# Own tiles for some early weights, own PSUM banks for the channel transform, and layer 1's first queries beside its latent keys

## Chip, core and metric

One core of one Trainium2 chip runs a forward pass of two layers in one launch. The metric is the device time of one execution in microseconds (us). Before the change the median of three runs is 1389.44 us (1386.45 to 1392.38).

## What is computed

Each of the two layers takes 256 latent tokens `x` and 256 context tokens `xc` of width 1024, in fp32:

```python
h = modulate(x, g_norm1, sh1, sc1)          # rms_norm * (1 + scale) + shift, from silu(c) @ w_mod
proj = h @ w_in                             # keys/values (288+ cols), queries, Fourier input, three gates
o_mla  = attention(q_mla, k_mla, v_mla)     # 8 heads, latent attention with a rotary key
o_gqa  = attention(q_gqa, k_gqa, v_gqa)     # 8 query heads on 2 key/value heads
o_four = real(fftn(f, axes=(tokens, channels of a group)))     # 4 groups of 128 channels
y = sig(g0)*(o_mla @ w_br_mla) + sig(g1)*(o_gqa @ w_br_gqa) + sig(g2)*(o_four @ w_four)
x = x + gt1 * (y @ w_o)
u = conv3(modulate(x, g_norm2, sh2, sc2) @ w_up)               # depthwise, width 3
x = x + gt2 * ((silu(a) * v) @ w_down)                         # a, v = halves of u
```

Context tokens go through the same weights with a constant conditioning vector; in layer 1 they only give keys and values. The output is `x` after layer 1.

## The kernel before

Activations lie feature-major, 128 features of all tokens to a tile. An fp32 product is three matmuls of rounded halves, hi·hi, hi·lo and lo·hi (`mm3`, L107 to L110), so each weight has to be split into a high and a low part before TensorE (PE) can use it. `wchunk` (L77 to L103) does that. The SP queue loads up to 512 KB into one of three `raw` buffers, ScalarE (ACT) casts the high part (L122), and VectorE (DVE) subtracts it from the weight to give the low part (L128). The results go into rings of three tiles, `whi` and `wlo`. Where a call names tiles of its own (`own`), they go there, and the ring is left free for others. SP issues in order, so a load waits for its `raw` buffer and everything behind it waits too.

The order of the instructions on each engine is set by a scheduler that simulates a timeline from the program and its priorities. Engines then run their lists strictly in order, PE's included. PSUM tiles come from five named groups: `mm`, `s` and `pt` with two banks each, `o` and `tk` with one each.

Names, in the order of a layer (the prefix `L0` or `L1` is the layer):

- `norm_mod` (L329): squares (`sq`, ACT), sums over features by PE (`ss`, L360), a reciprocal root on DVE in a dozen small steps, a diagonal `dg` (L369), its broadcast by PE (`rb`, L370), and then per feature tile `t` (DVE, L375), `h` high (ACT, L376) and `h` low (DVE L381, for every fourth tile ACT L378 and POOL L379). Stats and apply run for the latent half of the columns first, then for the context half.
- `kvg` (L527 on): keys and values of four token tiles, 288 columns each. Layer 1 does the two latent tiles first, then `q_chunk(0)` with its weights in tiles of their own, then the two context tiles, then `q_chunk(1)` (256 columns each, tiles `qg`). `fo`/`fp` is the projection for Fourier mixing.
- `Zc`, `Zs` (L633 to L650): the transform over channels, two products per group `b`, put together into `z` by DVE (L642, L643) and ACT (L639, L644). In layer 0 all `Zc` use `mm` and all `Zs` use `s`.
- `gk` and `KG` (L844 to L848): transposes of the GQA keys and their copies for attention.
- Gates `gp`, branch products `bp` with weights `b_w`; `gM`, `bM` are those of the MLA branch. `yh` is the split of the gated sum, `o` the output projection with weights `wo`.
- ConvFFN: `upp`, then `dp` with weights `dn`, in two groups of 12 and 10 hidden tiles in layer 0. Layer 1's modulation vectors are computed in the meantime: `sums` (L1016) runs steps of `mod_sums` (L283), each a load of 512 KB of `w_mod` (`mraw`, two buffers) and one DVE multiply-add (`mod_acc`, L298).
- `mod_burst` (L242): a quarter of one modulation block as products on PE (`mod_ps`, L259). Layer 1 runs two of them ahead of its first norm's context half, in the list `n1`, and two at its second norm, in `n2`.
- `next_norm` (L1180): layer 1's norm, begun inside layer 0's last down projection.

## Time and profile before

| | us |
|---|---|
| median of three runs | 1389.44 (1386.45 to 1392.38) |
| profiled execution, its own time | 1388.23 |
| its span, first to last instruction | 1386.4 |
| PE busy (share of the span) | 1339.8 (97%) |
| DVE, ACT, POOL busy | 949.8 (69%), 660.7 (48%), 334.4 (24%) |
| mean granted TensorE clock | 0.988 of full speed |

Times inside the program are us from the span's start. "Busy" is time with an instruction in flight; a wait is idle time of an engine, put down to what came last before it went on. PEclk is the granted TensorE clock as a share of 2.4 GHz, so 0.50 is the level of 1.2 GHz.

### The profile page before, as it was taken

The page shows a single profiled execution, that of the slowest core. Times are in us where ns is not written, and L with a number is a line of the kernel's source. Part 1 is how long each engine was busy: PE and PEld are TensorE (multiplying, and loading weights), DVE is VectorE, ACT ScalarE, POOL GpSimd, SP SyncE. Part 2 cuts the span into 40 slices and gives each one's busy share as a digit, 9 for nine tenths or more (in the row PEclk, how much of TensorE's full clock was granted, in tenths as well). Part 3 has the DMA queues.
Part 4 walks back from the last instruction along what each step waited for, and adds up shares of the span by engine and source line. Part 5 has one row for each costly group of instructions (what it writes and reads, how often), then busy time and mean ns, then how long its engine had stood idle before and what let it go on. Part 6 is the DMA issues. An engine that isn't in the chain of part 4 may idle for free.

```text
span 1386.4 us, 22211 instructions
## 1 busy us (share of the span) xinstructions
PE 1339.8 (97%) x8381; PEld 1171.6 (85%) x8381; DVE 949.8 (69%) x1686; ACT 660.7 (48%) x1166; POOL 334.4 (24%) x399
## 2 busy tenths in 40 slices
PE   6999999999999999999999999899998999899998
PEld 4887888877888789888788888888987998899998
DVE  4675755676654657777966667778788867788853
ACT  3534654435454335444214443355665664566642
POOL 2211232264322421111000102121244524012200
PEclk8999999999999999999999999999999999999999
DMA  9733343234311633434673346644425346456663
GB/s 320 252 92 107 110 152 105 64 108 114 102 62 47 241 114 103 137 94 149 197 258 119 110 129 201 197 127 121 138 66 152 92 121 204 132 177 184 185 193 119
DMA packets 160437, 197.40 MB, mean 142 GB/s; under 512 B 7080, under 2 KB 144858, under 8 KB 160330
## 3 DMA queue, kind: packets, MB, share of 16 engines
q1 hardware_dynamic: 159328, 195.32, 45.4%
q8 instruction: 66, 1.08, 0.3%
q0 software_dynamic: 864, 0.61, 0.3%
q14 instruction: 41, 0.34, 0.1%
q10 hardware_dynamic: 138, 0.04, 0.0%
HBM read 191.76 MB, written 3.15 MB: 141 GB/s over the span
## 4 chain that ended last, share of the span: by engine, by line
PE 86%; DVE 6%; issue 3%; DMA 2%; POOL 2%; ACT 1%; SPq 0%; DVEq 0%; ACTq 0%; POOLq 0%
PE L0upp L109 6%; PE L0upp L108 6%; PE L0upp L110 6%; PE L1upp L108 3%; PE L1upp L109 3%; PE L1upp L110 3%; PE L0gp L109 3%; PE L0gp L110 3%; PE L0gp L108 3%; PE L0dp L108 2%; PE L0dp L109 2%; PE L0dp L110 2%; PE L1gp L110 2%; PE L1dp L110 2%; PE L1dp L109 2%
## 5 line engine op out<-in xcount | busy, mean ns | idle before, releaser
L108 PE MATMUL L0upp<-L0n_h,L0up_h 128*128 128x512 f32 (+1 forms) x384 | 141.5, 372 | 1.1 <-ACT L0n_h L376 1.1
L109 PE MATMUL L0upp<-L0n_h,L0up_h 128*128 128x512 f32 (+1 forms) x384 | 142.5, 373 | 0.0
L110 PE MATMUL L0upp<-L0n_h,L0up_l 128*128 128x512 f32 (+1 forms) x384 | 139.1, 371 | 0.0
L108 PE MATMUL L1upp<-L1n_h,L1up_h 128*128 128x256 f32 x352 | 97.0, 287 | 1.1 <-ACT L1n_h L376 1.1
L110 PE MATMUL L1upp<-L1n_h,L1up_l 128*128 128x256 f32 x352 | 97.1, 285 | 0.0
L109 PE MATMUL L1upp<-L1n_h,L1up_h 128*128 128x256 f32 x352 | 96.5, 285 | 0.0
L1065 POOL TENSOR_TENSOR L0sg<-L0sg,L0u 128x512 f32<-128x512 f32 x22 | 29.6, 1343 | 273.9 <-DVE L0u L1042 273.9
L108 PEld LDWEIGHTS L0upp<-L0n_h,L0up_h 128*128 128x128 f32 x384 | 71.9, 188 | 14.4 <-ACT L0n_h L376 1.5
L109 PEld LDWEIGHTS L0upp<-L0n_h,L0up_h 128*128 128x128 f32 x384 | 72.2, 188 | 13.0 <-DVE L0n_t L375 0.4
L110 PEld LDWEIGHTS L0upp<-L0n_h,L0up_l 128*128 128x128 f32 x384 | 72.3, 188 | 12.5
L128 DVE TENSOR_TENSOR L0up_l<-L0up_w,L0up_h 128x1024 fp32r<-128x1024 f32 x44 | 59.2, 1347 | 34.2 <-ACT L0up_h L122 33.7
L122 ACT CAST L0up_h<-L0up_w 128x1024 fp32r<-128x1024 f32 x44 | 46.4, 1054 | 75.4 <-PE L0upp L109 52.1
L108 PE MATMUL L0gp<-L0n_h,L0g_h 128*128 128x512 f32 x192 | 76.4, 399 | 0.0
L109 PE MATMUL L0gp<-L0n_h,L0g_h 128*128 128x512 f32 x192 | 76.2, 397 | 0.0
L298 DVE SCALAR_TENSOR_TENSOR mod_acc<-mod_w,cpad,mod_acc 128x1024 f32<-128x1024 f32 x49 | 62.9, 1308 | 18.6 <-DMA mod_w<-in_w_mod_dram 18.4
L110 PE MATMUL L0gp<-L0n_h,L0g_l 128*128 128x512 f32 x192 | 75.2, 398 | 0.0
L110 PE MATMUL L0dp<-L0act,L0dn_l 128*128 128x512 f32 (+1 forms) x196 | 72.5, 370 | 0.8 <-DVE L0dn_l L128 0.8
L108 PE MATMUL L0dp<-L0act,L0dn_h 128*128 128x512 f32 (+1 forms) x196 | 72.6, 371 | 0.0
L109 PE MATMUL L0dp<-L0act,L0dn_h 128*128 128x512 f32 (+1 forms) x196 | 72.1, 368 | 0.0
L108 PEld LDWEIGHTS L1upp<-L1n_h,L1up_h 128*128 128x128 f32 x352 | 67.3, 196 | 1.8 <-ACT L1n_h L376 1.8
L128 DVE TENSOR_TENSOR L1up_l<-L1up_w,L1up_h 128x1024 fp32r<-128x1024 f32 x44 | 54.5, 1238 | 19.2 <-ACT L1up_h L122 17.8
L110 PEld LDWEIGHTS L1upp<-L1n_h,L1up_l 128*128 128x128 f32 x352 | 67.3, 194 | 0.0
(1564 smaller groups left out, 4278.9 us busy)
## 6 DMA issues: line engine op xcount, KB each, us to landing
mod_w<-in_w_mod_dram SPq DMA_DIRECT2D x96, 512.0 KB, 4.8
L0up_w<-in_w_up_dram SPq DMA_DIRECT2D x44, 512.0 KB, 3.6
L1up_w<-in_w_up_dram SPq DMA_DIRECT2D x44, 512.0 KB, 4.3
L0g_w<-in_w_in_dram SPq DMA_DIRECT2D x24, 512.0 KB, 3.7
L1g_w<-in_w_in_dram SPq DMA_DIRECT2D x24, 512.0 KB, 3.7
L0dn_w<-in_w_down_dram SPq DMA_DIRECT2D x20, 512.0 KB, 4.0
L1dn_w<-in_w_down_dram SPq DMA_DIRECT2D x16, 512.0 KB, 3.6
L0wo_w<-in_w_o_dram SPq DMA_DIRECT2D x8, 512.0 KB, 7.2
```

The lines of the kernel that those rows point to most:

```text
L108: nc.tensor.matmul(ps, lh, rh, start=start, stop=False)
L109: nc.tensor.matmul(ps, lh, rl, start=False, stop=False)
L110: last_mm[0] = nc.tensor.matmul(ps, ll, rh, start=False, stop=stop).ins
L122: nc.scalar.copy(hi, src)
L128: ins = nc.vector.tensor_sub(lo, src, f(hi))
L298: nc.vector.scalar_tensor_tensor(acc, raw, cv, acc, op0=ALU.mult, op1=ALU.add)
L1065: nc.gpsimd.tensor_mul(g[:, :TQ], g[:, :TQ], us[1][:, :TQ])
```

## The change

Five things are changed in the code.

1. Layer 0's channel transform takes `pt`, `o` and `tk` for groups 2 and 3, beside `mm` and `s`.
2. The last of the four `bM` weights, the first `wo` chunk and half of the second get tiles of their own, `H0` to `H7`, which hold layer 0's first normed activations until the last gate has read them.
3. Layer 1's first query weights are loaded in `next_norm`, into `Y0`, `Y1` and the two `mraw` buffers. The first queries of both latent tiles are computed feature tile by feature tile beside the latent keys, in the two `pt` banks. `dg` moves to another tag, and the list of the ConvFFN's slots changes to fit.
4. All four bursts of layer 1's block 5 run at its second norm, with eight tiles of their own; none is left at the first.
5. In the second up group of layer 0 two steps of the modulation sums run per pair of hidden tiles, where it was one.

```diff
@@ wchunk (own tiles; an own part may now be None, or in the mod weights' pool)
-            if own:
-                hi, lo = (S.tile([P, WMAX], F32R, tag=t, name=f"{name}_{x}{i}") for x, t in zip("hl", own[len(parts)]))
+            if own and own[len(parts)]:
+                hi, lo = (wpool.tile([P, WMAX], F32R, tag=t, name=f"{name}_{x}{i}", bufs=2) if t == "mraw" else
+                          S.tile([P, WMAX], F32R, tag=t, name=f"{name}_{x}{i}") for x, t in zip("hl", own[len(parts)]))
...
@@ norm_mod, stats
-            dg = S.tile([P, 256], F32, tag=f"E{s}", name=f"{nm}_dg")
+            dg = S.tile([P, 512], F32, tag="of", name=f"{nm}_dg", bufs=2)[:, :256]
...
@@ layer, first projections
-            hs, seq, _ = norm
+            (hs, seq, _), wq0 = norm
...
+        def q_part(w, k, tt, ps):
+            ts = slice(tt * P, (tt + 1) * P)
+            wh, wl = w(k, 0, 256)
+            mm3(ps[:, :256], hs[k][:, 0, ts], hs[k][:, 1, ts], wh, wl, k == 0, k == KD - 1)
...
         for tts in ((0, 1), (2, 3)) if l else (range(4),):
+            psq = [pm(f"{n_}qg{tt}0", "pt") for tt in range(2)] if l and tts[0] == 0 else []
             for k in range(KD):
+                for tt, ps in enumerate(psq):
+                    q_part(wq0, k, tt, ps)
                 wh, wl = w3(k, 0, 288)
...
-            if l and tts[0] == 0:
-                q_chunk(0, ("pt", "pt"), [("B0", "B1"), ("B2", "D0")])
+            for tt, ps in enumerate(psq):
+                marks["qg0"] = wq0.last
+                q_done(0, tt, ps)
...
@@ layer, Fourier mixing
-            zc = pm(f"{n_}Zc{b}", "mm" if not last else "pt")[:, :260].rearrange("p (s k) -> p s k", s=2)
-            zs = pm(f"{n_}Zs{b}", "s" if not last else ("o", "tk")[b])[:, :256].rearrange("p (s k) -> p s k", s=2)
+            zc = pm(f"{n_}Zc{b}", "mm" if not last and b < 2 else "pt")[:, :260].rearrange("p (s k) -> p s k", s=2)
+            zs = pm(f"{n_}Zs{b}", ("s", "s", "o", "tk")[b + 2 * last])[:, :256].rearrange("p (s k) -> p s k", s=2)
...
@@ layer, merge and output projection
-            bM(mc, ("s", "mm", "pt", "s")[mc] if not last else ("s", "mm")[mc % 2])
+            bM(mc, ("s", "mm", "pt", "s")[mc] if not last else ("s", "mm")[mc % 2],
+               [("H0", "H1")] if mc == 3 and not last else None)
...
-            wos.append(wchunk(a["w_o"][l], 0, KD, mc * 256, 256, f"{n_}wo{mc}"))
+            wos.append(wchunk(a["w_o"][l], 0, KD, mc * 256, 256, f"{n_}wo{mc}",
+                              None if last else ([("H2", "H3"), ("H4", "H5")], [("H6", "H7"), None])[mc]))
...
@@ layer, ConvFFN
-        slots = ["B0", "B1", "B2", "B3", "D0", "D1", "D2", "D3", "D4", "Y0", "Y1", "E0", "E1"]
+        slots = ["B0", "B1", "B2", "B3", "D0", "D1", "D2", "D3", "D4", "E0", "E1", "Y0"]
...
-                    sums(1)
+                    sums(2 if j0 else 1)
...
@@ next_norm and the second layer's call
-        return n1
+        return n1, wchunk(a["w_in"][1], 0, KD, 928, 256, "L1qg0", [("Y0", "Y1"), ("mraw", "mraw")])
...
-        "n1": bursts(1, 5, (0, 1), ["Y1", "Y2", "Y3", "E1"], "pt"), "g": [], "m": [],
-        "n2": bursts(1, 5, (2, 3), free[8:12], "pt"), "f": [], "v": []}, [], None, nxt[0])
+        "n1": [], "g": [], "m": [], "n2": bursts(1, 5, range(4), free[8:], "pt"), "f": [], "v": []}, [], None, nxt[0])
```

What the scheduler makes of it, at three places. Line numbers in the rows of the change are those of the changed file, 1 to 14 higher.

ACT's list in layer 0's channel transform, before. `z` is the transform's result (L644 reads `Zc`, the buffer number tells the group), `KG` the GQA keys.

```order
L122 CAST L0fo_1224<-L0z_1220 128x512
L847 CAST L0KG_1279<-L0gk 64x512
L848 CAST L0KG_1279<-L0gk 64x512
L847 CAST L0KG_1280<-L0gk 64x512
L848 CAST L0KG_1280<-L0gk 64x512
L644 COPY L0z_1237<-L0Zc_1227 128x4
L639 COPY L0zt_1269<-L0Zs_1262 128x256
L644 COPY L0z_1254<-L0Zc_1244 128x4
```

After:

```order
L123 CAST L0fo_1224<-L0z_1220 128x512
L656 COPY L0z_1237<-L0Zc_1227 128x4
L651 COPY L0zt_1269<-L0Zs_1262 128x256
L123 CAST L0fo_1241<-L0z_1237 128x512
L656 COPY L0z_1254<-L0Zc_1244 128x4
L123 CAST L0fo_1258<-L0z_1254 128x512
L656 COPY L0z_1271<-L0Zc_1261 128x4
L123 CAST L0fo_1275<-L0z_1271 128x512
L859 CAST L0KG_1279<-L0gk 64x512
```

The key copies stood between group 0's and group 1's `z`; now they stand behind all four groups.

DVE's list at the end of layer 0's merge, before. `b_l` is the low part of the last branch weight, `gt` the gated product, `wo_l` output weights, and `yh` the first operand of the output projection.

```order
L128 TENSOR_TENSOR L0b_l_4738<-L0b_w_4735,L0b_h_4737 128x1024
L592 SCALAR_TENSOR_TENSOR L0gt_4243<-L0gt_4243,L0bp_0_4705 128x512
L592 SCALAR_TENSOR_TENSOR L0gt_4243<-L0gt_4243,L0bp_1_4706 128x512
L172 COPY cw_4771<-cw_p 128x88
L128 TENSOR_TENSOR L0wo_l_4823<-L0wo_w_4820,L0wo_h_4822 128x1024
L128 TENSOR_TENSOR L0wo_l_4829<-L0wo_w_4826,L0wo_h_4828 128x1024
L130 SCALAR_TENSOR_TENSOR L0yh_4784<-L0y_523,L0yh_4784 128x512
```

After:

```order
L129 TENSOR_TENSOR L0wo_l_4843<-L0wo_w_4840,L0wo_h_4842 128x1024
L604 SCALAR_TENSOR_TENSOR L0gt_4243<-L0gt_4243,L0bp_0_4705 128x512
L604 SCALAR_TENSOR_TENSOR L0gt_4243<-L0gt_4243,L0bp_1_4706 128x512
L173 COPY cw_4771<-cw_p 128x88
L129 TENSOR_TENSOR L0wo_l_4955<-L0wo_w_4952,L0wo_h_4954 128x1024
L129 TENSOR_TENSOR L0wo_l_4961<-L0wo_w_4958,L0wo_h_4960 128x1024
L131 SCALAR_TENSOR_TENSOR L0yh_4784<-L0y_523,L0yh_4784 128x512
```

The last branch weight and the first three output weights have moved further up; three later output weights have come to stand ahead of the first `yh`.

ACT's list from the last steps of layer 0 to layer 1's first norm, before (`qg_h` query weights, `h` the normed activations):

```order
L122 CAST L1qg_h_8514<-L1qg_w_8512 128x1024
L263 COPY mod_row_8405<-mod_ps_8392 128x256
L348 ACTIVATE L1n_sq_8329<-L0x_4811 128x256
L348 ACTIVATE L1n_sq_8331<-L0x_4811 128x256
L376 ACTIVATE L1n_h_8104<-L1n_t_8165,modT_186 128x256
L376 ACTIVATE L1n_h_8105<-L1n_t_8169,modT_186 128x256
L376 ACTIVATE L1n_h_8106<-L1n_t_8173,modT_186 128x256
L122 CAST L1qg_h_8520<-L1qg_w_8518 128x1024
L376 ACTIVATE L1n_h_8107<-L1n_t_8177,modT_186 128x256
```

After, first at the end of the down projection, where the cast of the first query weights stands between two casts of down weights:

```order
L123 CAST L0dn_h_8015<-L0dn_w_8013 128x1024
L310 COPY mod_row_7942<-mod_ps_7937 128x256
L123 CAST L1qg_h_8201<-L1qg_w_8199 128x1024
L123 CAST L0dn_h_8021<-L0dn_w_8019 128x1024
L123 CAST L0dn_h_8027<-L0dn_w_8025 128x512
```

and then at the norm itself:

```order
L123 CAST L1kvg_h_8439<-L1kvg_w_8437 128x576
L349 ACTIVATE L1n_sq_8341<-L0x_4811 128x256
L349 ACTIVATE L1n_sq_8343<-L0x_4811 128x256
L377 ACTIVATE L1n_h_8104<-L1n_t_8165,modT_186 128x256
L377 ACTIVATE L1n_h_8105<-L1n_t_8169,modT_186 128x256
L377 ACTIVATE L1n_h_8106<-L1n_t_8173,modT_186 128x256
L377 ACTIVATE L1n_h_8107<-L1n_t_8177,modT_186 128x256
L377 ACTIVATE L1n_h_8108<-L1n_t_8182,modT_186 128x256
```

Query casts no longer stand between the steps of the norm. On PE the products of queries and keys now alternate there by feature tile.

## Rows read from the trace of the kernel before

**Rows 1.** The page: busy time by engine; the chain that ended last, by engine

```profile
PE 1339.8 (97%) x8381; PEld 1171.6 (85%) x8381; DVE 949.8 (69%) x1686; ACT 660.7 (48%) x1166; POOL 334.4 (24%) x399
...
PE 86%; DVE 6%; issue 3%; DMA 2%; POOL 2%; ACT 1%; SPq 0%; DVEq 0%; ACTq 0%; POOLq 0%
```

**Rows 2.** PE's waits, whole span (for what: us in total, times, longest us)

```profile
PE L1kvg L108 <- ACT L1n_h L376: 2.6, 2, 1.4
...
PE L0Zc L108 <- ACT L0z L644: 2.6, 1, 2.6
...
PE L1n_rb L370 <- DVE L1n_dg L369: 2.2, 1, 2.2
...
PE L0o L109 <- DVE L0yh L130: 2.0, 1, 2.0
...
PE L0bp L110 <- DVE L0b_l L128: 1.8, 2, 1.2
...
PE L1kvg L110 <- POOL L1n_h L379: 1.5, 1, 1.5
...
PE L0dp L110 <- DVE L0dn_l L128: 0.8, 1, 0.8
```

**Rows 3.** Windows at L0's channel transform (the first row names the columns)

```profile
core 0: us, PE busy (x) PEld busy (x) DVE busy (x) ACT busy (x) POOL busy (x), PEclk, DMA share, GB/s
...
104.60:107.20 2.60, 0.02 (x1) 0.00 (x0) 1.53 (x4) 2.54 (x7) 0.00 (x0) 1.00 0.00 0
107.20:110.60 3.40, 3.37 (x9) 2.82 (x10) 3.24 (x6) 1.86 (x6) 1.58 (x2) 0.50 0.00 0
```

**Rows 4.** ACT by line, 103.5 to 107.3 (xcount, busy us, mean ns, idle before)

```profile
L848 ACT CAST L0KG<-L0gk 64x512 fp32r<-64x512 f32 x2 | 1.2, 580 | 0.0
```

**Rows 5.** Windows at the start of L0's output projection

```profile
462.70:465.40 2.70, 0.69 (x4) 0.32 (x2) 2.70 (x3) 2.06 (x3) 2.10 (x1) 1.00 0.92 330
465.40:469.00 3.60, 3.60 (x9) 2.81 (x10) 3.60 (x7) 0.07 (x1) 1.17 (x1) 0.53 1.03 320
```

**Rows 6.** DVE by line, 453.5 to 466

```profile
L128 DVE TENSOR_TENSOR L0wo_l<-L0wo_w,L0wo_h 128x1024 fp32r<-128x1024 f32 x2 | 4.4, 2254 | 0.0
...
L128 DVE TENSOR_TENSOR L0b_l<-L0b_w,L0b_h 128x1024 fp32r<-128x1024 f32 x1 | 2.0, 2009 | 0.0
```

**Rows 7.** DVE by line, 872 to 882.1

```profile
L298 DVE SCALAR_TENSOR_TENSOR mod_acc<-mod_w,cpad,mod_acc 128x1024 f32<-128x1024 f32 x3 | 4.3, 1440 | 1.7 <-DMA mod_w<-in_w_mod_dram 1.7
```

**Rows 8.** Windows from L0's last down product to L1's Fourier projection

```profile
890.90:895.20 4.30, 3.13 (x32) 2.14 (x31) 4.30 (x9) 3.56 (x8) 0.00 (x0) 1.00 0.57 190
895.20:900.70 5.50, 4.15 (x20) 3.91 (x19) 3.00 (x11) 1.69 (x4) 0.00 (x0) 0.69 1.01 312
900.70:907.90 7.20, 5.63 (x31) 5.40 (x32) 5.72 (x17) 3.40 (x8) 1.77 (x2) 0.76 0.39 112
...
920.00:929.20 9.20, 9.20 (x76) 9.20 (x75) 5.45 (x19) 4.49 (x9) 3.43 (x8) 1.00 0.54 142
```

**Rows 9.** ACT's waits, 888 to 906

```profile
ACT L1qg_h L122 <- DMA L1qg_w<-in_w_in_dram: 4.6, 2, 3.8
```

**Rows 10.** PE by line, 890 to 930

```profile
L259 PE MATMUL mod_ps<-mod_w,cpad 128*32 128x256 f32 x32 | 2.1, 385 | 0.0
```

**Rows 11.** Windows at L1's second norm

```profile
1181.30:1185.70 4.40, 1.91 (x19) 1.66 (x15) 3.79 (x17) 0.25 (x1) 0.00 (x0) 1.00 0.75 237
1185.70:1192.60 6.90, 5.78 (x24) 5.07 (x25) 5.49 (x14) 3.63 (x8) 0.73 (x1) 0.51 0.01 3
```

**Rows 12.** DVE by line, 1182 to 1186

```profile
L266 DVE TENSOR_TENSOR mod_row<-mod_row,mod_ps 128x256 f32<-128x256 f32 x2 | 0.8, 417 | 0.1
```

**Rows 13.** DMA issues, 885 to 905 (xcount, KB each, median us to landing)

```profile
L1qg_w<-in_w_in_dram SPq DMA_DIRECT2D x4, 512.0 KB, 4.5
```

**Rows 14.** The page's costliest groups: two whole-chunk weight splits

```profile
L128 DVE TENSOR_TENSOR L0up_l<-L0up_w,L0up_h 128x1024 fp32r<-128x1024 f32 x44 | 59.2, 1347 | 34.2 <-ACT L0up_h L122 33.7
...
L122 ACT CAST L0up_h<-L0up_w 128x1024 fp32r<-128x1024 f32 x44 | 46.4, 1054 | 75.4 <-PE L0upp L109 52.1
```

More of the change, by code (lines that the diff above doesn't have):

```diff
@@ L583, in gate, with branch @@
                          whole=lambda ps: nc.scalar.activation(packed[mc], ps, AF.Tanh, scale=0.5))
-            def branch(mc, bank=bank):
-                w = wchunk(a[wname][l], 0, 4, mc * 256, 256, f"{n_}b{b}{mc}")
+            def branch(mc, bank=bank, own=None):
+                w = wchunk(a[wname][l], 0, 4, mc * 256, 256, f"{n_}b{b}{mc}", own)
                 def gated(g, y, ps):
```

26 lines of the change are left out of this document (13 added, 13 removed).

## The prediction

> **What bounds the kernel now.** I read the page first. PE is busy for 97% of the span, and 86% of the chain that ended last is PE's [rows 1]. So a gain can come from three things only: products taken away, time in which PE stands idle, and time in which it runs at 1.2 GHz instead of 2.4. The change takes no products away, it only moves some. PE's waits come next. No single one is long. The places that the change touches show 2.6 us at layer 0's channel transform, 1.2 (the longer of two) and 2.0 at layer 0's merge and output projection, 0.8 in the last down projection, 2.6 and 1.5 at layer 1's keys, and 2.2 at layer 1's second norm [rows 2]. The windows then show what follows such a wait. After the 2.6 us at the transform, PE is busy for 3.37 of 3.40 us at a granted clock of 0.50 [rows 3]. Such a stretch delivers half its products, so it costs 1.7 us on top of the wait. The same shows after the wait at the output projection (0.53, [rows 5]), in two stretches at layer 1's keys (0.69 and 0.76, [rows 8]) and after its second norm (0.51, [rows 11]). So each wait is priced twice, as idle time and as clock.
>
> The profiled execution took 1388.23 us, of which 1386.4 are the span. The median of the runs is 1389.44, 1.2 above it. The sum is made on the trace and then taken off the median.
>
> **Part by part.**
>
> *Channel transform.* PE waits for L644, an ACT copy of four columns, and PE's own list is not at fault. Ahead of that copy on ACT stand the four key copies: the two of L848 take 0.58 each, those of L847 as much, together 2.3 us [rows 4]. The product that waits needs the bank which that copy frees. With banks of its own no group waits for another group's copy, and the key copies come behind all four `z`. The gain is at most 2.6 of wait and 1.7 of clock, 4.3. It is nothing at all if the first gate, which takes the next bank, waits instead. I take −3.5. PE gets 24 products and a gate without a stop, but the gate's first bank is still freed by ACT, which now has 2.3 us of key copies right behind, and I keep 0.8 for that.
>
> The Trainium skill speaks against it. In "TensorE: Matmul & The Clock Gate", in the section on how the clock oscillation bites in real kernels, a kernel whose products were already put in one run gained nothing further from PSUM double-buffering. By that page this part is 0 and the time 1381.6. The trace differs in one point, that the wait here ends with the copy that frees a bank [rows 2].
>
> *Merge and output projection of layer 0.* The last branch weight is split earlier, so the 1.2 us wait for `b_l` goes. But PE then only reaches the output projection sooner, and that waits for the first `yh`, which stands on DVE behind big splits. Before these were one `b_l` of 2.01 and two `wo_l` of 2.25 [rows 6]. Now they are three later `wo_l`. So the first `yh` is ready when it was, and the 2.0 us wait becomes 3.2. I take 0. The ends are −1.2 (`yh` comes earlier by that much) and +1.7 (the longer wait lengthens the stretch at half clock by one more). On SP seven `wo` loads now go ahead of the reloads of `x`. Those are first needed when a whole output group is done, and both kinds of load wait for tiles that come free earlier, so I cost that at nothing.
>
> *Last down projection.* Two steps of the modulation sums per pair of tiles bring the sums to an end earlier. DVE's `mod_acc` steps of 1.44 us [rows 7] then no longer stand ahead of the last down weights, and 0.8 of wait goes. A new wait comes: on ACT the copy of a modulation row, which needs a product at the end of the third quarter, now stands ahead of the cast of the first query weights, and that ahead of the fourth quarter's second down weights. Two casts of 1.05, and the split of 1.35 on DVE behind them [rows 14], with the copy (some 0.4, an estimate from the 256-column step of [rows 12]) make 3.9 us. The products in front that hide them are 24 of 256 columns, at 9.20/76 = 0.121 us each [rows 8] 2.9. So 1.0 shows. The term is +0.2, between −0.8 and +2.0 (both casts and the split bare).
>
> *Start of layer 1.* From 890.9 to 929.2 it takes 38.3 us [rows 8]. There PE has 96 query products of 256 columns, 0.121 each, 11.6 us, and 96 key products of 288 columns, by columns 0.136 (an estimate), 13.1. Two bursts of 2.1 us together [rows 10] leave. What the wait rows show is that ACT, in the middle of the norm, holds the cast of the second query weights and waits 3.8 us for their load [rows 9]. The activations behind it, and so PE, wait with it. In the new list that cast stands before the norm, its load goes ahead of most others, and each feature tile has 12 products (1.5 us) in place of 6. A DVE step on 256 columns takes 0.42 [rows 12] and a tile needs two, 0.84, so PE should set the pace once it has begun. Up to the first product there were 4.3 us, now 3.2 without the burst. The sum is 11.6 + 13.1 + 3.2, with one stretch at half clock (1.7, there were two) and the second half's broadcast (0.3), 29.9. So −8.4. The ends are −10.1 (no such stretch) and −2.1 (only the bursts leave, the norm sets the pace as before). The key weights are now loaded behind the queries, two of the context copies and the transform tables. They still have the down projection's fourth quarter to arrive, 120 products of 0.121, some 14 us, so I cost that at nothing. Without that cover a load costs up to 4.5 [rows 13].
>
> *Second norm of layer 1.* The two bursts come back here, 2.1 us. They stand behind the sums of squares and ahead of the broadcast, where PE is idle for 2.2 [rows 2] and is busy for 1.91 of 4.40 [rows 11]. They fill it. But DVE has two of the row additions inside its chain of small steps where both of the two stood ahead of it, each 0.42 [rows 12]. I take +0.4. The ends are −1.7 (PE no longer falls idle and half of the stretch at 0.51 goes) and +2.1 (nothing is hidden). Their loads, eight in place of four, go between the last branch weights on SP. Two tiles come free with each of the last two heads' scores, so SP is not held up long.
>
> *ConvFFN slots and the diagonal's tag* change no instruction's cost: 0.
>
> **Sum:** −3.5 + 0 + 0.2 − 8.4 + 0.4 = −11.3, 1376.9 for the profiled execution, 1378.1 for the median. All best ends together give −18.1, so 1371.
>
> **Rivals.**
>
> *The banks give nothing.* The wait moves to the first gate's bank: then −7.8, 1381.6. For it speaks that ACT is as busy there as it was (2.54 of 2.60 [rows 3]). Against it, the gate needs the bank only after all 24 products. By the skill's page above it would be so.
>
> *Query weights hold up the down projection.* The first of their two loads may start only when DVE has split the fourth quarter's first down weights, and if the sums' steps still stand there, it lands after that quarter has begun. Then ACT waits with the down weights behind it. A whole load of 4.5 [rows 13] and a stretch at half clock of 1.7 make +6.2, 1384. For it: the cast stands between two down casts. Against it: the sums are meant to end earlier.
>
> *Slower: attention of layer 0 runs out of cover.* The key copies go behind the transform, so the eight GQA heads start later, between gates and branch products as before, and yet have to be done by the same place. Where a head's softmax finds too few products beside it, PE waits. The nearest row is the wait in this same stretch, 2.6 and 1.7 of clock, 4.3 a head [rows 2, 3]. With three heads the gain is eaten (12.9 against 11.3), with four it is 1395. For it: every step of attention stands behind the moved copies. Against it: PE's table has no wait for layer 0's GQA heads among its larger ones, so there is cover to lose.
>
> **How the numbers follow.** A measurement of this kernel can tell about 0.5%, 6.9 us, from no change, so faster is below 1382.5. The forecast gets 0.62, the banks 0.12 (split about evenly by that line), the held-up down projection 0.14 (same), attention 0.05 (slower). Of the 0.07 left, in which the start of layer 1 gains little, nearly all is no change. That is 0.69 faster, 0.25 same, 0.06 slower. The range goes from 1371 to 1386, which takes in the second rival with the upper end of the merge's term.
>
> **What would show it.** The transform's wait on L644 is gone and the clock stays at 1.00 from 100 to 112. PE's wait for the first `yh` is over 3 us. The way from the last down product to the first Fourier product is near 30 us with at most one stretch at half clock, and ACT shows no wait for query weights within it. The second norm's wait is under 1 us. The forecast is wrong if the last down projection shows a wait of several us for down weights, if layer 1's keys and queries still wait for `h` at each tile, or if GQA heads of layer 0 appear in PE's waits.

## The result and the profile after

The changed kernel takes 1373.59 us (median of four runs, 1373.26 to 1375.59), beside 1389.09 for the kernel before in the same comparison (1386.45 to 1392.38). The ratio is 0.9894, with a 95% interval of 0.9877 to 0.9911. The time fell by 15.5 us where 11.3 were forecast, and lies in the range given, 1371 to 1386. The profiled execution has a span of 1371.5 us, 14.9 below that of before.

The page of the changed kernel, busy time by engine and the chain that ended last, by engine (as [rows 1]):

```profile
PE 1334.1 (97%) x8381; PEld 1168.4 (85%) x8381; DVE 949.2 (69%) x1686; ACT 660.1 (48%) x1166; POOL 335.0 (24%) x399
...
PE 89%; DVE 6%; DMA 2%; POOL 1%; issue 1%; ACT 1%; SPq 0%; ACTq 0%; DVEq 0%; POOLq 0%
```

PE has the same 8381 products, and its busy time fell by 5.7 us (1339.8 to 1334.1). A PE that does the same work in less busy time ran less of it at half clock. The rest of the gain is waiting that went.

PE's waits in the changed kernel, whole span (for what: us in total, times, longest us), as [rows 2]:

```profile
PE L0o L110 <- DVE L0yh L131: 3.5, 1, 3.5
...
PE L1n_ss L361 <- ACT L1n_sq L349: 1.1, 2, 0.7
...
PE L0gp L109 <- ACT L0gt L594: 1.1, 1, 1.1
...
PE mod_ps L275 <- DVE mod_row L267: 0.5, 1, 0.5
...
PE L1n_rb L371 <- DVE L1n_dg L370: 0.4, 1, 0.4
```

Gone are the 2.6 for `L0z`, the 1.2 for `b_l`, the 0.8 for `dn_l`, and all waits for `L1n_h` at layer 1's keys. The wait for `L1n_rb` fell from 2.2 to 0.4. That for the first `yh` rose from 2.0 to 3.5, and one is new, 1.1 for a gate's `gt`.

Windows of the changed kernel (the first row names the columns): the transform, as [rows 3]; the new wait of 1.1; the output projection, as [rows 5]; the start of layer 1, as [rows 8]; its second norm, as [rows 11]:

```profile
core 0: us, PE busy (x) PEld busy (x) DVE busy (x) ACT busy (x) POOL busy (x), PEclk, DMA share, GB/s
101.10:103.70 2.60, 2.60 (x23) 2.55 (x22) 2.52 (x5) 2.17 (x6) 0.00 (x0) 1.00 0.17 59
103.70:107.10 3.40, 3.38 (x19) 2.76 (x18) 3.38 (x9) 2.52 (x8) 0.00 (x0) 1.00 0.00 0
250.50:252.80 2.30, 1.27 (x11) 1.09 (x9) 1.11 (x9) 1.08 (x2) 0.36 (x1) 1.00 0.00 0
...
459.40:463.00 3.60, 0.20 (x2) 0.00 (x0) 3.60 (x3) 1.14 (x2) 3.05 (x2) 1.00 0.97 329
463.00:466.90 3.90, 3.84 (x10) 3.05 (x11) 3.90 (x6) 0.75 (x2) 1.66 (x1) 0.57 1.01 330
886.97:891.30 4.33, 3.20 (x21) 2.72 (x20) 4.33 (x10) 3.02 (x8) 0.00 (x0) 0.87 0.55 151
891.30:896.80 5.50, 5.50 (x37) 5.50 (x37) 5.40 (x23) 3.19 (x7) 0.74 (x1) 0.79 0.36 101
896.80:904.00 7.20, 7.20 (x58) 7.15 (x57) 3.84 (x11) 2.81 (x8) 1.02 (x2) 1.00 0.00 0
904.00:916.50 12.50, 12.50 (x101) 12.50 (x100) 9.84 (x29) 8.49 (x20) 6.47 (x11) 1.00 0.39 112
1168.50:1173.00 4.50, 3.56 (x46) 2.37 (x45) 3.83 (x18) 0.34 (x2) 0.00 (x0) 1.00 0.72 230
1173.00:1180.00 7.00, 5.88 (x44) 5.38 (x45) 5.96 (x16) 4.05 (x9) 0.74 (x1) 1.00 0.01 2
```

At the transform the 3.4 us that held 9 products at 0.50 now hold 19 at 1.00, with no idle time ahead. After the second norm 7.0 us hold 44 products at 1.00, where 6.9 held 24 at 0.51. The start of layer 1 keeps one dip, 0.87 and 0.79 in a row, and PE is never idle from 891.3 on. Of these places only the output projection still shows the old picture, a wait and then 10 products in 3.9 us at 0.57.

**Where the 15 us went.** PE works through its list in order, so the start of the same product in two traces tells how far one is ahead. The table gives, for every kernel of this study, how much longer (+) or shorter (−) a stretch between two such products is than in the changed kernel. The stretches are: up to the last key product of layer 0 (*start-up*); from there to the first gate product (*transform*); to the last `ukv` product (*latent*); to the last product of the output projection (*merge*); to layer 0's last `dp` (*down*); to the first `L1fp` (*L1 start*); to the first `L1upp` (*L1 rest*); to the last `L1upp` (*norm 2*). So *L1 rest* takes in the second norm itself, and *norm 2* is the up projection right behind it. What comes after it is equal in all of them to 0.05.

| kernel | start-up | transform | latent | merge | down | L1 start | L1 rest | norm 2 | sum |
|---|---|---|---|---|---|---|---|---|---|
| before | −0.6 | +4.1 | −0.9 | −0.1 | +1.3 | +9.0 | +0.3 | +1.9 | +15.0 |
| z_alone | −1.3 | 0 | 0 | −0.2 | +1.6 | +9.6 | +0.1 | +2.2 | +12.1 |
| bursts_alone | −0.6 | +4.0 | −0.8 | −0.1 | +1.1 | +3.7 | +1.3 | 0 | +8.4 |
| two_edits | −0.3 | 0 | 0 | −0.1 | +2.3 | +3.6 | +1.5 | 0 | +7.0 |
| z_undone | −0.3 | +3.9 | −0.8 | −0.1 | +1.6 | +0.2 | +1.5 | 0 | +6.0 |
| own_undone | −2.5 | 0 | 0 | −0.1 | +0.5 | +1.5 | +1.4 | 0 | +0.9 |
| sums_undone | −1.8 | 0 | 0 | −0.1 | +6.2 | +0.2 | +0.4 | +1.1 | +6.0 |
| bursts_back | +0.2 | 0 | 0 | −1.9 | −0.1 | +3.2 | +2.7 | +2.4 | +6.4 |
| q_behind | −2.5 | 0 | 0 | 0 | −0.1 | 0 | 0 | 0 | −2.6 |
| q_forced | −1.4 | 0 | +0.1 | −0.2 | +0.1 | +0.5 | +0.3 | 0 | −0.6 |
| q_late | −2.9 | 0 | +0.6 | −0.2 | 0 | +1.0 | +1.6 | 0 | +0.1 |
| yh_first | +0.4 | 0 | +1.6 | −4.9 | +0.1 | 0 | +0.3 | 0 | −2.6 |
| best | +0.2 | 0 | −1.1 | −4.1 | +0.1 | +2.4 | +0.3 | 0 | −2.2 |

The start-up differs by up to 3.3 us from trace to trace, and no edit touches it. So a total of one execution is worth little here, and the stretches are what the experiments are read by. They have a limit too: behind the same waits PE's clock is not the same in every execution, which by itself moves a stretch by up to some 2 us (the last section).

### The profile page after: what moved, and what is told of

Read it like the earlier page. It is cut to its first block, busy times and chain, and to the rows that moved or that the text cites. A ratio compares the mean times of both kernels' runs of the same rounds, so it can differ in the third digit from the quotient of the medians.

```text
span 1371.5 us, 22227 instructions
## 1 busy us (share of the span) xinstructions
PE 1334.1 (97%) x8381; PEld 1168.4 (85%) x8381; DVE 949.2 (69%) x1686; ACT 660.1 (48%) x1166; POOL 335.0 (24%) x399
## 4 chain that ended last, share of the span: by engine, by line
PE 89%; DVE 6%; DMA 2%; POOL 1%; issue 1%; ACT 1%; SPq 0%; ACTq 0%; DVEq 0%; POOLq 0%
PE L0upp L109 6%; PE L0upp L110 6%; PE L0upp L111 6%; PE L1upp L109 3%; PE L1upp L110 3%; PE L1upp L111 3%; PE L0dp L109 3%; PE L0dp L111 3%; PE L0dp L110 3%; PE L0gp L109 3%; PE L0gp L111 3%; PE L0gp L110 3%; PE L1dp L111 2%; PE L1dp L110 2%; PE L1dp L109 2%; PE L0bp L111 1%
## 5 line engine op out<-in xcount | busy, mean ns | idle before, releaser
L1079 POOL TENSOR_TENSOR L0sg<-L0sg,L0u 128x512 f32<-128x512 f32 x22 | 29.6, 1345 | 274.1 <-DVE L0u L1056 274.1
L109 PEld LDWEIGHTS L0upp<-L0n_h,L0up_h 128*128 128x128 f32 x384 | 71.9, 188 | 14.3 <-ACT L0n_h L377 1.5
L110 PEld LDWEIGHTS L0upp<-L0n_h,L0up_h 128*128 128x128 f32 x384 | 72.2, 188 | 13.0 <-DVE L0n_t L376 0.4
L129 DVE TENSOR_TENSOR L0up_l<-L0up_w,L0up_h 128x1024 fp32r<-128x1024 f32 x44 | 59.2, 1348 | 32.1 <-ACT L0up_h L123 31.6
L109 PEld LDWEIGHTS L1upp<-L1n_h,L1up_h 128*128 128x128 f32 x352 | 65.9, 192 | 1.5 <-ACT L1n_h L377 1.5
L110 PEld LDWEIGHTS L1upp<-L1n_h,L1up_h 128*128 128x128 f32 x352 | 66.2, 192 | 0.1
```

The lines of the kernel that those rows point to most:

```text
L109: nc.tensor.matmul(ps, lh, rh, start=start, stop=False)
L110: nc.tensor.matmul(ps, lh, rl, start=False, stop=False)
L129: ins = nc.vector.tensor_sub(lo, src, f(hi))
L1079: nc.gpsimd.tensor_mul(g[:, :TQ], g[:, :TQ], us[1][:, :TQ])
```

## Experiments

### The channel transform's banks

**z_alone**, on the kernel before:

```diff
-            zc = pm(f"{n_}Zc{b}", "mm" if not last else "pt")[:, :260]...
-            zs = pm(f"{n_}Zs{b}", "s" if not last else ("o", "tk")[b])[:, :256]...
+            zc = pm(f"{n_}Zc{b}", "mm" if not last and b < 2 else "pt")[:, :260]...
+            zs = pm(f"{n_}Zs{b}", ("s", "s", "o", "tk")[b + 2 * last])[:, :256]...
```

> The kernel before with the banks of the channel transform alone (groups 2 and 3 in `pt`, `o` and `tk`). Theory (the banks take the 2.6 us wait and the stretch at half clock behind it): PE shows no wait for `L0z`, the clock stays at 1.00 from 100 to 112, the first gate product starts at 104.6 where it was 108.0, and the execution takes about 1385.2, 3.1 less than 1388.2. Rival (the wait moves to the first gate's bank, or double-buffering gives nothing): the first gate product starts at 107 to 108 and the time is within 1 us of 1388. A second question: in the changed kernel a wait of 1.1 for the gate's `gt` stands at 251.8. If the banks alone bring it (the key copies behind the transform shift the later order), it shows here too and the gain at the first latent query product is 2.5; if another part of the change brings it, it is absent and the gain there is 3.5.

It took 1385.35 us, with a span of 1383.5. Its window at the transform, where the wait and the half clock were:

```profile
102.40:105.80 3.40, 3.37 (x19) 2.75 (x18) 3.37 (x9) 2.52 (x8) 0.00 (x0) 1.00 0.00 0
```

Among PE's waits, whole span:

```profile
PE L0gp L108 <- ACT L0gt L582: 1.1, 1, 1.1
```

And ACT's longest wait from 240 to 256:

```profile
ACT L0cqsq L723 <- PE L0ckss L735: 3.8, 1, 3.8
```

The first gate product comes 51.1 us after the last key product, as in the changed kernel, and 55.2 in the kernel before. So the banks take 4.1 from this stretch, nearly all of the 4.3 that the wait and the stretch at half clock cost. They bring the wait of 1.1 too. ACT's row tells how. It stands for 3.8 us before a square of the latent queries (`cqsq`) whose buffer PE has not yet read out (it is one of three that the key squares have before it, and `ckss` are the sums of these), and the gate's `gt`, for which PE waits, is behind that square on ACT. PE stops for a bank that ACT is to free, with ACT waiting for PE. The net gain at the last `ukv` is 3.1.

**z_undone**, the same two lines put back in the changed kernel:

> The changed kernel with the channel transform in `mm` and `s` alone, as before. Theory (the term is its own, independent of the others): the wait of 2.6 for `L0z` is back, with a stretch at about 0.5 of the clock, the first gate product starts at 108.0, the 1.1 at 251.8 is gone, and the execution takes 2.5 to 3.5 more than the changed kernel's 1373.6, about 1376.7. Rival (what is lost here is made up later, because the attention of layer 0 has slack that ends at the same place): the way up to the last GQA head is later by 3 but the output projection of layer 0 starts within 1 us of 458.9.

It took 1379.26 us. Its windows at the transform:

```profile
104.80:107.40 2.60, 0.13 (x2) 0.00 (x0) 1.42 (x4) 2.54 (x7) 0.00 (x0) 1.00 0.00 0
107.40:110.80 3.40, 3.26 (x10) 2.68 (x11) 3.32 (x6) 1.86 (x7) 1.58 (x2) 0.55 0.00 0
```

PE's waits, at the transform and in the last down projection:

```profile
PE L0Zc L109 <- ACT L0z L656: 2.6, 1, 2.6
...
PE mod_ps L307 <- DVE mod_acc L299: 1.0, 1, 1.0
```

The wait of 2.6 and the stretch at half clock (0.55) are back. The term is its own: +3.9 and −0.8, 3.1 net, and nothing of it is made up before the output projection. The total is 5.7 over the changed kernel's, where 3.5 at most was expected. The difference lies far from the edit: 1.6 in the down projection, where PE waits 1.0 for the modulation sums (the second row) after DVE has waited 2.6 for one of their loads (0.3 in the changed kernel), and 1.5 in the rest of layer 1, of which the last section tells.

### The tiles of their own in layer 0's merge

**own_undone**, on the changed kernel:

```diff
-               [("H0", "H1")] if mc == 3 and not last else None)
+               None)
...
-                              None if last else ([("H2", "H3"), ("H4", "H5")], [("H6", "H7"), None])[mc]))
+                              None))
```

> The changed kernel without tiles of their own for the last branch weight of layer 0 and the first output weights. Theory (the two waits trade places): the wait of 1.2 for `b_l` is back, the wait for the first `yh` falls from 3.5 to about 2.0, and the last output product comes within 0.5 us of where it was: 1373.6, give or take 0.7. Rival (the own tiles cost what the longer `yh` wait shows): 1.5 faster, 1372.1. Second rival (they are worth the `b_l` wait): 1.2 to 2.9 slower, up to 1376.5.

It took 1374.12 us. PE's waits from 440 to 520:

```profile
PE L0o L110 <- DVE L0yh L131: 2.0, 1, 2.0
PE L0bp L111 <- DVE L0b_l L129: 1.2, 1, 1.2
```

The two waits trade places to a tenth: the first output product comes 1.3 later against the stretch's start, the last one 0.1 earlier. By themselves these own tiles gain nothing here. They move a wait from the branch weight to `yh`. The 1.5 and 1.4 more at the start and in the rest of layer 1 come mostly from the clock, behind waits of the same length in all (the last section).

### Two steps of the sums per pair of tiles

**sums_undone**, on the changed kernel:

```diff
-                    sums(2 if j0 else 1)
+                    sums(1)
```

> The changed kernel with one step of the modulation sums per pair of hidden tiles in both up groups, as before. Theory (ending the sums earlier is what took the two waits of 0.8 and 0.3 out of the last down projection): those waits come back, the way from the first to the last down product is longer by about 1.3, and the time is 1374.9. Rival (the cast of the first query weights now waits for the `mraw` buffers that the sums still hold, with down weights behind it): 4 to 6 more, 1378 to 1380, with a wait for `dn` of several us. Second rival (the waits went because layer 1's query weights took `Y0`, `Y1` and with them the ConvFFN's slots changed): no difference, 1373.6 within 0.5.

It took 1379.31 us. PE's waits from 870 to 892:

```profile
PE L1n_ss L361 <- POOL L1n_sa L354: 1.9, 1, 1.9
PE L0dp L109 <- DVE L0x L982: 1.1, 1, 1.1
PE L0dp L111 <- DVE L0dn_l L129: 0.3, 1, 0.3
```

The windows around them:

```profile
875.00:878.50 3.50, 1.94 (x13) 1.43 (x11) 3.41 (x6) 1.61 (x3) 1.67 (x3) 1.00 0.95 306
878.50:880.30 1.80, 0.04 (x1) 0.04 (x1) 1.80 (x3) 0.25 (x2) 1.80 (x2) 0.59 0.76 236
880.30:884.00 3.70, 3.70 (x19) 2.66 (x20) 0.11 (x1) 1.00 (x3) 0.59 (x1) 0.50 0.51 151
```

The down projection is 6.2 longer. That is 3.3 of waits and the rest mostly clock, with only 19 products in 3.7 us at 0.50. The price is that of the prediction's rival in which query weights hold up the down projection (+6.2), but ACT's waits for them say little: 4.3 before the first cast here, 4.2 in the changed kernel. The form is another, too: the down weights cost 0.3, and most comes from DVE, where two steps of the sums (1.3 each, at 874.0 and 877.0) stand among the residual's additions, for which PE and the norm's squares wait. So with the early query weights the sums must end earlier. Part of the 6.2 is there without those weights as well: the kernel before, with late weights and one step per pair, is 1.3 longer in this stretch, while `q_late` below, with late weights and two steps, is as short as the changed kernel. That comparison has the other edits in it, the ConvFFN's slots above all, and the steps were not tried alone on the kernel before.

### The start of layer 1

Four parts changed here: where the bursts stand, when the query weights come, in which order the queries are written, and how early their two `pt` banks are taken.

**bursts_back**, on the changed kernel:

```diff
-        "n1": [], "g": [], "m": [], "n2": bursts(1, 5, range(4), free[8:], "pt"), ...
+        "n1": bursts(1, 5, (0, 1), ["B0", "B1", "B2", "D0"], "pt"), "g": [], "m": [],
+        "n2": bursts(1, 5, (2, 3), free[8:12], "pt"), ...
```

> The changed kernel with two of block 5's four bursts again ahead of the context half of layer 1's first norm, and two at its second norm. Theory (at the first norm PE has too little time free for them, at the second they stand in its idle time): the way from the last down product to the first Fourier product goes from 29.6 to 31.7 (the 2.1 us of the two bursts in full), the wait for `L1n_rb` goes from 0.4 to about 2.2, with one stretch at half clock more, and the time is 1373.6 + 2.1 + 2.0 = 1377.7. Rival (at the first norm they now hide behind the feature tiles, and the second norm's gain has another cause): both places within 0.7 of the changed kernel, 1374.

It took 1379.67 us. PE's waits at the second norm, and, second row, at the start of layer 1:

```profile
PE L1n_rb L371 <- DVE L1n_dg L370: 2.2, 1, 2.2
...
PE mod_ps L260 <- DMA mod_w<-in_w_mod_dram: 1.4, 2, 0.7
```

The window behind the first:

```profile
1177.00:1184.00 7.00, 5.88 (x26) 5.48 (x27) 5.86 (x14) 4.02 (x9) 0.73 (x1) 0.56 0.01 3
```

Both places move the way the theory had it: the wait of 2.2 and the half clock (0.56) are back at the second norm, whose up products take 2.4 longer, and the start of layer 1 is 3.2 longer. That is the bursts' 2.1 and 1.1 more. PE waits 1.4 for their weights there and 0.4 for `L1n_h`, but no longer the 1.1 for the squares, which is 0.7 of it. The total is about 2 above the theory's: 1.1 and 0.4 at these two places, 2.7 more in the rest of layer 1 and 1.9 less in the merge.

**q_behind** and **q_late**, each on the changed kernel. The first writes the queries behind the latent keys, the second loads their weights in layer 1, into `B0`, `B1`, `B2`, `D0`, and leaves them interleaved:

```diff
-            psq = [pm(f"{n_}qg{tt}0", "pt") for tt in range(2)] if l and tts[0] == 0 else []
-                for tt, ps in enumerate(psq):
-                    q_part(wq0, k, tt, ps)
-            for tt, ps in enumerate(psq):
+            for tt in range(2) if l and tts[0] == 0 else ():
+                ps = pm(f"{n_}qg{tt}0", "pt")
+                for k in range(KD):
+                    q_part(wq0, k, tt, ps)
```

> The changed kernel with layer 1's first queries computed behind the latent keys, not feature tile by feature tile beside them; their weights stay early. Theory (the interleaving is what covers the norm's pace, 12 products per feature tile where the keys alone have 6): PE waits for `L1n_h` again, 2.6 to 4.1 in all, with one or two stretches at half clock (1.7 each): 29.6 becomes 34 to 37, and the time 1378 to 1381. Rival (the early weights did it, since ACT no longer stops for their load in the middle of the norm): `L1n_h` waits of at most 1 us, 29.6 to 31, the time within 1.5 of 1373.6.

```diff
+        if l:
+            wq0 = wchunk(w_in, 0, KD, 928, 256, f"{n_}qg0", [("B0", "B1"), ("B2", "D0")])
...
-        return n1, wchunk(a["w_in"][1], 0, KD, 928, 256, "L1qg0", [("Y0", "Y1"), ("mraw", "mraw")])
+        return n1, None
```

> The changed kernel with the first queries still interleaved with the latent keys, but their weights loaded in layer 1, into tiles that come free with the last down projection. Theory (early weights are needed for the interleaving): ACT has the two casts of 1.05 and DVE two splits of 1.35 between the norm's steps, PE waits for `qg` weights by 3 to 6 and runs a stretch at half clock: 29.6 becomes 34 to 38, the time 1378 to 1382. Rival (interleaving alone does it, the load lands in time): within 1.5 of 1373.6, and the down projection has the same length.

Both theories fell and both rivals hold at the place itself. `q_behind` took 1370.66 us and `q_late` 1373.39, and at the start of layer 1 they are 0.0 and 1.0 longer than the changed kernel; neither waits for `L1n_h`. The first result says nothing about interleaving, though. PE's list shows that the scheduler puts the queries between the keys whatever order they are written in, as soon as their weights and banks are there. Its list in `q_behind`, in the first feature tile:

```
L109 MATMUL L1kvg_8444<-L1kvg_h_8427,L1n_h_8104 128x288
L110 MATMUL L1kvg_8444<-L1kvg_l_8428,L1n_h_8104 128x288
L109 MATMUL L1qg_8495<-L1qg_h_8201,L1n_h_8104 128x256
L110 MATMUL L1qg_8495<-L1qg_l_8202,L1n_h_8104 128x256
L109 MATMUL L1qg_8524<-L1qg_h_8201,L1n_h_8104 128x256
```

**q_forced**, on the changed kernel, therefore holds them back with an order edge from the last latent key product (`q_behind`, with the products in `with tc.issue_after(lk):`, where `lk` is that product).

> The changed kernel, weights early, with the first queries of both latent tiles held back on PE until the last latent key product. (In the run in which they only were written behind the keys, PE's list still had them between the keys, since they were ready.) Theory (12 products per feature tile cover the norm's pace, 6 do not): PE waits for `L1n_h` by 2.5 to 4 in all with a stretch at half clock (1.7), 29.6 becomes 33 to 36. Rival (it is the early weights and the missing bursts; the keys alone keep PE busy, the norm is fast enough once ACT has no casts in it): 29.6 to 30.6, waits under 1 us.

It took 1372.63 us. PE's waits from 884 to 925:

```profile
PE L1n_ss L361 <- ACT L1n_sq L349: 1.1, 2, 0.7
PE L1kvg L111 <- DVE L1n_h L382: 0.3, 1, 0.3
```

Those of `q_late` from 883 to 920:

```profile
PE L1n_ss L361 <- ACT L1n_sq L349: 1.5, 1, 1.5
PE L1n_rb L371 <- DVE L1n_dg L370: 1.0, 1, 1.0
```

With all queries behind all latent keys the start of layer 1 takes 30.0 us, 0.5 more, and PE waits 0.3 for `L1n_h`. So the rival stands: six products per feature tile keep PE busy too, and the interleaving is worth half a microsecond here. Late weights cost 1.0 net: PE is idle for 1.6 more, while its clock stays at 1.00 where the changed kernel has the dip. Neither is more than the clock alone adds to this stretch in `own_undone` (1.5) or `best` (2.0 of its 2.4), so both are prices of one execution and not resolved.

**bursts_alone**, on the kernel before:

```diff
-        "n1": bursts(1, 5, (0, 1), ["Y1", "Y2", "Y3", "E1"], "pt"), "g": [], "m": [],
-        "n2": bursts(1, 5, (2, 3), free[8:12], "pt"), "f": [], "v": []}, [], None, nxt[0])
+        "n1": [], "g": [], "m": [],
+        "n2": bursts(1, 5, range(4), free[8:], "pt"), "f": [], "v": []}, [], None, nxt[0])
```

> The kernel before with all four bursts of block 5 at layer 1's second norm, and nothing else of the change. Theory (the start of layer 1 gained by the queries' own early weights and their place beside the keys; the bursts took only their own 2.1 us there): 38.3 becomes 36.2 from the last down product to the first Fourier product, 2.0 more come off at the second norm, and the time is 1388.2 - 4.1 = 1384.1. Rival (the bursts were what held the queries back: they occupied the two `pt` banks in which the first queries are summed, and their four loads stood ahead of the query weights; without them PE's list has the queries between the latent keys though nothing else is changed): 38.3 becomes 30 to 32, and with the second norm the time is 1378 to 1380.

It took 1381.7 us. PE's waits from 888 to 930:

```profile
PE L1n_ss L360 <- ACT L1n_sq L348: 1.9, 1, 1.9
PE L1qg L109 <- DVE L1qg_l L128: 1.6, 2, 0.9
```

ACT's for the query weights from 886 to 906, as [rows 9]:

```profile
ACT L1qg_h L122 <- DMA L1qg_w<-in_w_in_dram: 1.2, 2, 0.6
```

The start of layer 1 falls from 38.6 us to 33.2, and the second norm is as in the changed kernel. That lies between the two expectations, nearer to the rival. Of the 5.3 gained, 2.1 are the bursts themselves. The other 3.2 they had held up. ACT's wait for query weights fell from 4.6 to 1.2, but not for the bursts' loads: in the kernel before the last of these ahead of the queries is issued at 882.1, the first query load at 888.6, and here that load goes out at the same time (888.4). SP's wait in the kernel before, from 880 to 900, shows what it was:

```profile
SPq L473 <- PE mod_ps L259: 3.0, 1, 3.0
```

L473 copies `x` into `xk`, in the tiles `Y2` and `Y3`. The first burst's weights lie in `Y2` until its products have read them, so the copies wait, and the load of the second query weights stands behind them on SP. It is issued at 894.1; here, with the copies out of the way by 885, at 891.2. PE's list, too, has the queries between the keys, with no other edit, where in the kernel before they come behind the second burst, at 913. How much of the 3.2 goes to the load and how much to PE's order was not tried apart. No wait for `L1n_h` is left. What remains to the changed kernel, 3.7, is 2.4 of wait (3.5 here, for weights and the norm's squares, against 1.1) and 1.3 that no wait shows.

### Two edits

**two_edits** is the kernel before with the edits of `z_alone` and `bursts_alone`.

> The kernel before with two parts of the change: the banks of the channel transform and all four bursts at the second norm. Theory (these two carry the change; own tiles, early query weights and the faster sums add nothing or pay only for each other): about 1375.5, within 2.5 of the changed kernel's 1373.6. Rival (early weights and interleaving are worth more than half of the 9.0 at the start of layer 1): 1380 to 1382.

It took 1379.13 us (median of four, 1376.90 to 1380.28), ratio to before 0.9927 with an interval of 0.9912 to 0.9942. Both expectations missed: the two edits carry about 9 of the 15.5 us (1388.43 to 1379.13 in this comparison), and not nearly all. What they lack stands in the table, 2.3 in the down projection (a wait of 1.8 for `dn_l`), 3.6 at the start of layer 1, 1.5 in the rest of it. The last is mostly the clock. So what they leave out, the early weights, the banks taken ahead for the queries, the faster sums, the slots and the own tiles, earns about 6 in the first two (2.3 and 3.6), though the early weights undone alone cost 1. The down projection does not need them: in `q_late` the weights are late and it is as short as in the changed kernel. Whether the faster sums or the slots do it was not tried apart.

### Two waits that the change left or brought

**yh_first**, on the changed kernel:

```diff
             split(yT[m], y[:, 0, :TQ], y[:, 1, :TQ], 0.5)
+            if m == 3:
+                marks["yh3"] = marks["split"]
...
-            w = wchunk(a["w_o"][l], 0, KD, mc * 256, 256, f"{n_}wo{mc}")
+            with after("yh3", l == 0 and mc == 2):
+                w = wchunk(a["w_o"][l], 0, KD, mc * 256, 256, f"{n_}wo{mc}")
```

> The changed kernel with DVE's splits of the third output weight chunk of layer 0 put behind the first four `yh` splits; nothing else is moved. Theory (the 3.5 us wait for the first `yh` is DVE's order alone: its inputs are there at 455, two splits of 2.2 stand ahead of it): the wait falls under 0.5, the stretch at half clock behind it goes (1.7), and the time falls by 3.5 to 5.2, to about 1369.3. Rival (the wait moves: to the later `yh`, which need POOL's sums, or to the third chunk's weights): 0 to 1.5 less, with a new PE wait between 459 and 485.

It took 1370.48 us (median of four, 1368.97 to 1371.32), ratio to before 0.9865, interval 0.9844 to 0.9887. Its windows at the start of the output projection:

```profile
460.90:463.60 2.70, 2.70 (x14) 2.17 (x14) 2.70 (x3) 0.71 (x2) 2.70 (x3) 1.00 0.84 244
463.60:470.00 6.40, 6.40 (x30) 5.31 (x29) 6.40 (x8) 1.19 (x2) 2.90 (x2) 1.00 0.91 302
```

PE no longer stops and stays at full clock. The merge is 4.9 shorter, 3.5 of wait and 1.4 of clock, and no wait takes its place. The latent stretch of this execution is 1.6 longer, by the clock alone (the last section). The median is 3.1 below the changed kernel's, a little less than the 3.5 to 5.2 expected, and the two sets of runs, each beside its own runs of the kernel before (1389.09 and 1389.68), do not overlap. So the wait that the forecast took for the price of the own tiles was DVE's order alone.

**best** adds, in layer 0, another tag for the third `cqsq`:

```diff
-                    sq = S.tile([P, 512], F32, tag="gate", name=f"{n_}{nm}sq{i}", bufs=3)
+                    sq = (S.tile([P, 512], F32, tag="E0", name=f"{n_}{nm}sq{i}") if i == 2 and not l else
+                          S.tile([P, 512], F32, tag="gate", name=f"{n_}{nm}sq{i}", bufs=3))
```

> The changed kernel with two waits taken out that it brought or lengthened: DVE's splits of the third output weight chunk behind the first four `yh` splits (as in the run before, where it took 5.0 us), and layer 0's third query square in a tile of another tag, so that it need not wait for PE's sums of the key squares while the gate's `gt` is queued behind it. Theory: no wait at 251 (1.1 less, and up to 1.6 where it had brought a stretch at half clock), and no wait over 0.5 for `L0yh`: 5.0 and 1.0 less than the changed kernel, about 1367.6. Rival (the wait at 251 moves to the products behind the gate, which need the queries' root of the squares): 1368.6, as with the splits alone.

It took 1370.77 us (median of four, 1368.21 to 1371.09), ratio to before 0.9863, interval 0.9846 to 0.9879. The wait at 251 is gone and the latent stretch 1.1 shorter, but the time is that of `yh_first`, above both expectations. In the trace, other stretches gave it back: 0.9 of the 4.9 in the merge, and 2.4 at the start of layer 1, where PE's waits are 0.4 more and the clock stayed low for longer. Its lowest window:

```profile
886.00:890.00 4.00, 4.00 (x19) 4.00 (x19) 3.97 (x16) 1.93 (x6) 0.72 (x1) 0.50 0.52 153
```

Both versions beat the changed kernel by about 3 us. Whether the second edit adds anything these runs cannot tell.

## Why the prediction was right, term by term

The time came 4.5 us below the one forecast (1373.6 against 1378.1), within the range, and none of the rivals happened. The sum held better than some of the reasons. The terms below are read from the table.

- **Channel transform**, −3.5. The stretch itself gave 4.1 of the 4.3 at most. The first gate did not stop, for which 0.8 had been kept. But 0.9 came back almost 150 us further on, at a place that the prediction did not look at, so the net is −3.1. The mechanism is shown by both runs on the banks. The Trainium skill tells in "TensorE: Matmul & The Clock Gate" (the section on how the clock oscillation bites in real kernels) of a kernel with its products in one run, to which PSUM double-buffering gave no further gain; taken as a rule, that would have had 0 here. The measurement decides against it for this kernel, with 2.6 us of wait for a copy that a bank removes.
- **Merge and output projection**, 0. Measured 0.1, with the longer `yh` wait (3.5, forecast 3.2) and the `b_l` wait trading places, as `own_undone` shows. Right, but the term stopped at the trade: nothing but two splits on DVE held `yh`, and putting them behind it was worth 5.
- **Last down projection**, +0.2, measured −1.3, below the lower end of −0.8. The step that failed is "So 1.0 shows". The copy of the modulation row was put ahead of the query cast as part of the chain, but in the trace it is done by 866.7, and ACT then stands idle for 4.2 until the query weights land at 870.9. From there to the end of the split of the second down weights are 3.4 us, 874.3, and PE first needs them at 874.4. It fits by a tenth, so nothing of the 1.0 shows. And the 0.8 of wait for `dn_l` was not all there was to gain: the 0.3 that PE waited there for `mod_acc` is gone too. The gain is not safe: in `z_undone`, where DVE waits 2.3 more for a load of the sums, PE waits 1.0 for them and the stretch is no shorter than before the change.
- **Start of layer 1**, −8.4, measured −9.0, 29.6 us where 29.9 were forecast (29.3 if counted like the forecast, from 0.2 us after the last down product's start). The size was right, its division was not. The prediction gave the bursts their own 2.1 and put the lower end there ("only the bursts leave, the norm sets the pace as before"), and the rest to query casts out of the norm and to 12 products per tile. The runs show 5.3 for the bursts alone, and 1.0 for early weights and 0.5 for interleaving when each is taken alone out of the full change, both within what the clock does there by itself. What was missed is that the bursts held two more things: the tile that the copies of `x` wait for, with the second query weights behind these copies on SP, and the place ahead of the queries on PE.
- **Second norm of layer 1**, +0.4, measured −1.9. This is the term most off, beyond its own end of −1.7. The row additions inside DVE's chain did what the forecast said: the broadcast starts 6.8 us after the last output product where it started 6.5 after it, 0.3 later (forecast 0.4), and the bursts' 2.1 fill the wait, as forecast. PE's waits ahead of the broadcast are 0.5 for `mod_row` and 0.4 for `dg`, in place of 0.3 and 2.2. The step that failed is that the sum kept the stretch at half clock behind the norm, and the best end took off only half of it: with PE no longer idle ahead, the clock stays at 1.00, and the up products behind the norm take 1.9 less (*norm 2*). `bursts_back` returns the 2.2, the 0.56 and 2.4 us.

In this order the terms erred by 0.4, 0.1, 1.5, 0.6 and 2.3. The two largest errors are a delay that was priced in full and found cover, and a stretch at half clock that was kept though the wait ahead of it was taken to be filled. The two stretches that had no term differ by +0.6 (*start-up*) and −0.3 (*L1 rest*).

## What to carry to other kernels

When work is moved away from a place, list what it held there (banks, buffers, places in a load queue, places ahead on an engine) and not only its own duration: here the bursts' 2.1 us held up 3.2 more, part of it by a tile for which a whole load queue stood still. A wait that changes places is not yet a wait removed; ask which single instruction stands ahead of the late one and whether it is needed first, since putting two splits behind `yh` took 4.9 us out of its stretch, where the edit that had exposed them took nothing. Where parts of a change pay for each other, undoing one alone can cost nothing or far more than it gains, so try the small subset on the old kernel too.

## What the runs showed beside that

**The same wait need not bring the same clock.** In layer 0, `bursts_back` and the changed kernel have the same instructions and the same wait of 3.5 for the first `yh`. In the 3.9 us behind it the changed kernel does 10 products at 0.57 (above), `bursts_back` 17 at 1.00, which is the −1.9 in its merge:

```profile
PE L0o L110 <- DVE L0yh L131: 3.5, 1, 3.5
...
462.80:466.70 3.90, 3.85 (x17) 3.19 (x18) 3.90 (x5) 0.74 (x2) 1.67 (x1) 1.00 0.95 337
```

The same shows at layer 1's output projection, with the same waits to a tenth (1.5, the longest 1.2 and 1.1). The first row is of `q_late`, the second of the changed kernel:

```profile
1142.40:1145.90 3.50, 2.81 (x13) 2.81 (x14) 3.50 (x7) 0.00 (x0) 1.85 (x1) 0.59 0.49 154
```

```profile
1143.50:1147.00 3.50, 2.79 (x21) 2.64 (x22) 3.50 (x7) 0.00 (x0) 1.84 (x1) 1.00 0.50 154
```

That is some 1.1 of the 1.3 to 1.6 under "L1 rest" of five kernels. At the start of layer 1, `own_undone` has the products and the wait of the changed kernel (1.1) and takes 1.5 more; in its slowest 5.5 us it does 27 products, where the changed kernel does 37 at 0.79 (891.30, above):

```profile
889.20:894.70 5.50, 5.50 (x27) 5.50 (x27) 5.40 (x23) 3.19 (x7) 0.73 (x1) 0.52 0.36 101
```

Two more entries of the table are of this kind: the 1.6 in the latent stretch of `yh_first`, where behind the wait of 1.1 at 251 the clock is 0.54 for 3.5 us and in the changed kernel 1.00, and the 1.1 under "norm 2" of `sums_undone`. The prediction took 1.7 of clock for such a stretch; it comes in some executions and not in others. What decides it in one and not the other stays open.

**The first 54 us vary more than any later stretch that no edit touches.** The last key product of layer 0 starts at 50.7 us in `q_late` and at 53.9 in `yh_first`, and the 51 us behind it, up to the first gate product, then agree to 0.02 in all kernels with the new banks. The last products of these keys, first in `q_late`, then in `yh_first` (last two numbers: first and last start):

```profile
L111 PE MATMUL L0kvg<-L0kvg_h,L0n_h x32: 288/295/442, 26.2 to 50.7; 128*128 128x288 f32 x32
```

```profile
L111 PE MATMUL L0kvg<-L0kvg_h,L0n_h x32: 288/295/445, 28.4 to 53.9; 128*128 128x288 f32 x32
```

The products are as long (295 ns), they only begin 2.2 us later and end 3.2 later. The 1370.66 of `q_behind` comes from such a start and not from its edit.
